# 17 of 22 gate and up pairs of each feed-forward block as 2x2 block products of seven, in a two-layer hybrid decoder

## The chip, the cores and the metric

The kernel runs on one core of one Trainium2 chip. The metric is the device time of one execution in microseconds. All data are float32; matrix products run on TensorE, elementwise work on VectorE and ScalarE, a little on GpSimd.

## The reference

512 tokens with 1024 channels go through two layers. Each layer has a feed-forward block with half weight, a mixer (state space, sliding-window attention and spatial gating side by side) and a second feed-forward block. The change is in the four feed-forward blocks alone:

```python
def rmsnorm(x, w):
    y = x * lax.rsqrt(jnp.mean(x * x, axis=-1, keepdims=True) + EPS)
    return y * w
def swiglu(x, w_gate, w_up, w_down):          # (1024, 2816), (1024, 2816), (2816, 1024)
    return (jax.nn.silu(x @ w_gate) * (x @ w_up)) @ w_down
for l in range(DEPTH):                        # DEPTH = 2
    x = x + 0.5 * swiglu(rmsnorm(x, ffn1_norm[l]), ffn1_w_gate[l], ffn1_w_up[l], ffn1_w_down[l])
    ...                                       # the mixer
    x = x + 0.5 * swiglu(rmsnorm(x, ffn2_norm[l]), ffn2_w_gate[l], ffn2_w_up[l], ffn2_w_down[l])
return rmsnorm(x, final_norm)
```

## The kernel before

The residual stays in SBUF as eight tiles xT of 128 channels by 512 tokens. A weight product takes both operands as an exact pair hi + lo of numbers of the type float32r and sums hi*hi, hi*lo and lo*hi in PSUM (`product`, lines 148, 149 and 151): three matmuls with 128 x 128 weights and 512 moving columns for each chunk of 128 input channels.

`ffn` (line 252) splits the 2816 hidden channels into 22 tiles of 128. For each one `load` brings 512 KB of gate weights and 512 KB of up weights through SyncE's queue into one of five raw buffers; `split` parts them (cast on ScalarE, line 128, subtraction on VectorE, line 129) into one of four buffers each for hi and lo. `in_products` runs one product per tile over eight chunks: gate 0, up 0, gate 1, and so on. The first three tiles go through the chunks in levels, so that the last chunks of the residual may come late. The token scale R of the norm is not in the operand: `emit` multiplies the gate's product by R (line 302), takes silu (303), multiplies by the up product (307) and at once parts the result into the pair h (312, 313). In the last block the factor 0.5 R is applied here too (309). The down product then sums the 22 chunks of h for each of eight output tiles, `scalar_tensor_tensor` applies 0.5 R (333), and the result is added to xT (334). The last block's `down_final` (702) has tokens on partitions: the residual enters by 64 matmuls with an identity (710), then groups of two hidden tiles follow (722 to 724).

What the instructions need, and which buffers they may use, is traced by a framework; a planner orders what is ready on each engine, in the order of the program, and puts in the semaphores. Each engine then works its list in order. In the first block the weights and the residual come in a pinned order, the first four weight tiles through tiles of their own (`early`). GpSimd adds the squares for the norm's statistics at the start of each block.

## Time and profile before

| | us |
|---|---|
| median of 3 runs (lowest, highest) | 1886.74 (1886.61, 1889.0) |
| profiled execution: its time, which the profile gives as the span | 1886.8 |
| TensorE busy | 1868.9 (99%) |
| weight load busy, beside it | 1527.5 (81%) |
| VectorE busy | 874.1 (46%) |
| ScalarE busy | 632.5 (34%) |
| GpSimd busy | 127.9 (7%) |

The span runs from the first instruction to the last. PE is TensorE, PEld its weight load, DVE VectorE, ACT ScalarE, POOL GpSimd, SP SyncE. Matmuls are pipelined, so their recorded durations overlap, and a busy TensorE says nothing of how fast it goes; the distance between starts does. The granted clock is a share of 2.4 GHz: 0.50 is 1.2 GHz.

### The profile page before, as it was taken

How to read it: one execution, taken by the hardware profiler on the slowest of the kernel's cores; microseconds unless marked ns; L12 is line 12 of the kernel's file. 1: busy time of each engine (PE TensorE's matmuls, PEld its weight loads, DVE VectorE, ACT ScalarE, POOL GpSimd, SP SyncE). 2: the span in 40 equal slices, each digit the busy share in tenths (PEclk: the TensorE clock that was granted, in tenths of full speed). 3: DMA queues.
4: the chain of work that ended last, by engine and by line, in shares of the span. 5: the costliest groups of instructions: out<-in, count | busy, mean ns of one | idle time of the engine just before them, and what ended most of it. 6: DMA issues, size and time to landing. Idle time of an engine off the chain costs nothing.

```text
span 1886.8 us, 21326 instructions
## 1 busy us (share of the span) xinstructions
PE 1868.9 (99%) x8608; PEld 1527.5 (81%) x8608; DVE 874.1 (46%) x1203; ACT 632.5 (34%) x854; POOL 127.9 (7%) x126
## 2 busy tenths in 40 slices
PE   8999999999999999999999999999999999999998
PEld 6888888877888888888888888887778888888886
DVE  6444433368855433433344344333787554444222
ACT  4323322247443322322223233223564432232112
POOL 2000000010221000000000000001102200000000
PEclk9999999999999999999999999999999999999999
DMA  5222333342222232233322323333422223223231
GB/s 210 100 100 90 98 92 93 97 141 70 79 87 99 91 101 99 89 92 99 102 91 99 101 91 93 92 90 110 123 89 69 90 90 101 96 94 101 79 100 45
DMA packets 54926, 182.78 MB, mean 97 GB/s; under 512 B 7211, under 2 KB 9196, under 8 KB 54828
## 3 DMA queue, kind: packets, MB, share of 16 engines
q1 hardware_dynamic: 49484, 172.37, 28.2%
q0 software_dynamic: 1920, 6.59, 1.2%
q10 hardware_dynamic: 3424, 2.46, 0.4%
q8 instruction: 68, 1.11, 0.2%
q14 instruction: 30, 0.25, 0.0%
HBM read 178.48 MB, written 2.92 MB: 96 GB/s over the span
## 4 chain that ended last, share of the span: by engine, by line
PE 94%; DVE 2%; DMA 1%; issue 1%; ACT 1%; POOL 0%; POOLq 0%; SPq 0%; ACTq 0%; DVEq 0%
PE accb L148 28%; PE accb L149 28%; PE accb L151 28%; PE mxb L723 1%; PE mxb L724 1%; PE mxb L722 1%; PE accb L723 1%; PE accb L722 1%; PE accb L724 1%; DMA acb<-arow 1%; PE mxb L179 1%; PE mxb L492 0%; PE mxb L192 0%; PE mxb L588 0%; PE mxb L641 0%
## 5 line engine op out<-in xcount | busy, mean ns | idle before, releaser
L148 PE MATMUL accb<-xhi,whi 128*128 128x512 f32 x1856 | 728.5, 393 | 5.9 <-ACT xhi L137 5.9
L149 PE MATMUL accb<-xlo,whi 128*128 128x512 f32 x1856 | 727.2, 392 | 0.5 <-DVE xlo L138 0.5
L151 PE MATMUL accb<-xhi,wlo 128*128 128x512 f32 x1856 | 726.5, 391 | 0.0
L128 ACT CAST whi<-raw 128x1024 fp32r<-128x1024 f32 (+1 forms) x322 | 333.1, 1037 | 1077.5 <-PE accb L149 619.3
L129 DVE TENSOR_TENSOR wlo<-raw,whi 128x1024 fp32r<-128x1024 f32 (+1 forms) x322 | 387.5, 1206 | 302.6 <-ACT whi L128 293.1
L148 PEld LDWEIGHTS accb<-xhi,whi 128*128 128x128 f32 x1856 | 350.0, 189 | 78.7 <-ACT xhi L137 6.1
L149 PEld LDWEIGHTS accb<-xlo,whi 128*128 128x128 f32 x1856 | 349.6, 188 | 75.1 <-DVE xlo L138 2.6
L151 PEld LDWEIGHTS accb<-xhi,wlo 128*128 128x128 f32 x1856 | 349.7, 188 | 73.1 <-issue 1.0
L148 PE MATMUL accb<-h,whi 128*128 128x512 f32 x528 | 208.0, 394 | 0.0
L151 PE MATMUL accb<-h,wlo 128*128 128x512 f32 x528 | 207.0, 392 | 0.0
L149 PE MATMUL accb<-h,whi 128*128 128x512 f32 x528 | 204.9, 388 | 0.0
L307 DVE TENSOR_TENSOR t<-accb,t 128x512 f32<-128x512 f32 x88 | 60.8, 691 | 273.3 <-PE accb L151 273.2
L302 DVE TENSOR_TENSOR t<-accb,R 128x512 f32<-128x512 f32 x88 | 60.5, 691 | 204.0 <-PE accb L151 203.9
L172 POOL TENSOR_TENSOR sqs<-sqs,sq 128x512 f32<-128x512 f32 x48 | 74.9, 1561 | 1118.9 <-ACT sq L171 1117.7
L151 PEld LDWEIGHTS accb<-h,wlo 128*128 128x128 f32 x528 | 99.1, 188 | 23.2
L149 PEld LDWEIGHTS accb<-h,whi 128*128 128x128 f32 x528 | 99.1, 188 | 22.2
L148 PEld LDWEIGHTS accb<-h,whi 128*128 128x128 f32 x528 | 99.3, 188 | 19.7
L313 DVE TENSOR_TENSOR h<-t,h 128x512 fp32r<-128x512 f32 x88 | 60.3, 685 | 3.4 <-ACT h L312 3.4
L312 ACT CAST h<-t 128x512 fp32r<-128x512 f32 x88 | 54.7, 621 | 19.1 <-DVE t L309 16.7
L303 ACT ACTIVATE t<-t 128x512 f32<-128x512 f32 x88 | 55.1, 627 | 3.8 <-DVE t L302 3.5
L333 DVE SCALAR_TENSOR_TENSOR t<-accb,R 128x512 f32<-128x512 f32 x24 | 16.6, 692 | 57.7 <-PE accb L151 57.7
L138 DVE SCALAR_TENSOR_TENSOR xlo<-xT,col,xhi 128x512 fp32r<-128x512 f32 x48 | 40.7, 866 | 2.4 <-ACT xhi L137 2.4
(203 smaller groups left out, 1088.9 us busy)
## 6 DMA issues: line engine op xcount, KB each, us to landing
raw<-in_ffn_w_gate_dram SPq DMA_DIRECT2D x86, 512.0 KB, 3.3
raw<-in_ffn_w_up_dram SPq DMA_DIRECT2D x86, 512.0 KB, 3.3
raw<-in_ffn_w_down_dram SPq DMA_DIRECT2D x48, 512.0 KB, 3.5
raw<-in_w_in_dram SPq DMA_DIRECT2D x40, 512.0 KB, 3.3
raw<-in_last_w_down_dram SPq DMA_DIRECT2D x22, 512.0 KB, 3.3
raw<-in_ffn_w_down_dram SPq DMA_DIRECT2D x24, 384.0 KB, 3.1
raw<-in_w_out_dram SPq DMA_DIRECT2D x16, 512.0 KB, 3.3
acb<-arow POOLq DMA_DIRECT2D x8, 512.0 KB, 6.1
```

Of the source, the lines that this page charges most:

```text
L128: pinned(nc.scalar.copy(out=hi[:, c], in_=raw[:, c]))
L129: pinned(nc.vector.tensor_tensor(out=lo[:, c], in0=raw[:, c], in1=hi[:, c].bitcast(F32), op=ALU.subtract))
L138: pinned(nc.vector.scalar_tensor_tensor(out=lo, in0=src, scalar=w, in1=hi.bitcast(F32), op0=ALU.mult, op1=ALU.subtract))
L148: nc.tensor.matmul(ps, whi[:, i, :], xh, start=(k == first), stop=False)
L149: mm = nc.tensor.matmul(ps, whi[:, i, :], xl, start=False, stop=(wlo is None and k == last))
L151: mm = nc.tensor.matmul(ps, wlo[:, i, :], xh, start=False, stop=(k == last))
L172: eng.tensor_tensor(out=self.s, in0=self.s, in1=q, op=ALU.add)
L302: nc.vector.tensor_tensor(out=t, in0=b, in1=R, op=ALU.mult)
L303: nc.scalar.activation(out=t, in_=t, func=AF.Silu)
L307: nc.vector.tensor_tensor(out=t, in0=b, in1=t, op=ALU.mult)
L312: nc.scalar.copy(out=hi, in_=t)
L313: nc.vector.tensor_tensor(out=lo, in0=t, in1=hi.bitcast(F32), op=ALU.subtract)
```

## The change

The normed residual and a pair of gate and up tiles form a 2 x 2 block product. The residual's blocks A have 256 tokens by 512 channels; the weights' blocks B are gate and up (128 columns each) by the two halves of the channels. Four quarter results come from seven block products of sums and differences of blocks, each of 4 chunks x 3 matmuls with 256 moving columns. The first five pairs (HEAD) stay as they were, ten plain tiles. While they run, `operands` makes the seven left factors, now with R in them, four times: for each it takes two chunks, makes sums in the scratch tile T and parts all 1792 columns. For each later pair `Seven` loads both weight tiles, makes four sums on VectorE (in T too) and parts four sources, three of 1024 columns and one of 512. The loop issues the blocks with these partings between them; the seventh block is held back until the next pair's first two blocks have gone out (`finish_last`). 0.5 R and silu go into h, which is kept as one float32 tile: eight in the block's own tiles, the rest in the 16 tiles of the residual's pairs. `split_h` parts h at the start of the down product, in the rooms that T, the operands and others leave (`room`). The down product takes its first four output tiles together, eight chunks of h at a time, and does the held-back block after the first three chunks; `down_final` does it after the first quarter of its residual. The first four weight tiles of the run use raw buffers, and the attention's bias table uses T.

```diff
-RAW, TB = 5, 3
+HEAD = 5
+KEEP = 8
...
+    def parts(src, hi, lo):
+        nc.scalar.copy(out=hi, in_=src)
+        nc.vector.tensor_tensor(out=lo, in0=src, in1=hi.bitcast(F32), op=ALU.subtract)
...
+            elif then:
+                nxt = then()
             emit(lead + n, b)
+        return nxt
...
+            def temp():
+                return ff.tile([P, 2048], F32, name="tmp", tag="T")
...
-                early = [ff.tile([P, 1024], F32, name=f"early{n}", tag=f"h{14 + n}") for n in range(4)]
+                early = [rawtile() for n in range(4)]
...
-            for f in range(KF):
+            for f in range(HEAD):
                 tiles += [maker(gv, f), maker(uv, f)]
             cur = {}
+            def htile():
+                n = len(h)
+                if n < KEEP:
+                    h.append(ff.tile([P, T], F32, name=f"h{n}", tag=f"h{n}"))
+                else:
+                    h.append(xp.tile([P, T], F32, name=f"h{n}", tag="xs", bufs=16))
+                return h[n]
...
+            lows, highs = [], []
+            def operands(c):
+                pair = ff.tile([P, 2, 7, 256], F32R, name=f"as{c}", tag=f"as{c}")
+                hi, lo = pair[:, 0], pair[:, 1]
+                v = temp()[:, 0:1792].rearrange("p (i n) -> p i n", n=256)
+                a11, a12, a22, s1, s2, s3, s4 = (v[:, i, :] for i in range(7))
+                a21 = s3
+                tt = nc.vector.tensor_tensor
+                for j, o in ((c, v[:, 0:6:5, :]), (c + 4, v[:, 1:3, :])):
+                    nc.vector.scalar_tensor_tensor(out=o, in0=xT[j].rearrange("p (s n) -> p s n", s=2),
+                                                   scalar=vcol(wrow + j), in1=R.rearrange("p (s n) -> p s n", s=2),
+                                                   op0=ALU.mult, op1=ALU.mult)
+                tt(out=s1, in0=a21, in1=a22, op=ALU.add)
+                tt(out=s3, in0=a11, in1=a21, op=ALU.subtract)
+                tt(out=s2, in0=a11, in1=s1, op=ALU.subtract)
+                tt(out=s4, in0=a12, in1=s2, op=ALU.add)
+                parts(v, hi, lo)
+                lows.append(lo)
+                highs.append(hi)
             def emit(n, b):
                 if n % 2 == 0:
-                    t = ff.tile([P, T], F32, name="t", tag="t", bufs=TB)
+                    t = ttile32()
                     nc.vector.tensor_tensor(out=t, in0=b, in1=R, op=ALU.mult)
                     nc.scalar.activation(out=t, in_=t, func=AF.Silu)
                     cur[0] = t
+                    if n >= 2 and n // 2 <= 4:
+                        operands(n // 2 - 1)
                 else:
                     t = cur[0]
                     nc.vector.tensor_tensor(out=t, in0=b, in1=t, op=ALU.mult)
-                    if fin:
-                        nc.vector.scalar_tensor_tensor(out=t, in0=t, scalar=0.5, in1=R, op0=ALU.mult, op1=ALU.mult)
-                    pair = ff.tile([P, 2, T], F32R, name=f"h{len(h)}", tag=f"h{len(h)}")
-                    hi, lo = pair[:, 0, :], pair[:, 1, :]
-                    nc.scalar.copy(out=hi, in_=t)
-                    nc.vector.tensor_tensor(out=lo, in0=t, in1=hi.bitcast(F32), op=ALU.subtract)
-                    h.append((hi, lo))
+                    nc.vector.scalar_tensor_tensor(out=htile(), in0=t, scalar=0.5, in1=R, op0=ALU.mult, op1=ALU.mult)
                     if first and len(h) == 2:
-                        attention_bias(ff, ("h13", "h12", "h11"))
+                        bias = temp()
+                        attention_bias(lambda i: bias[:, i * 512:(i + 1) * 512])
...
-            in_products(tiles, xs, emit, {(3, 1) if first else (1, 0): st.start, (3 if first else 1, "R"): make},
-                        [[0, 1], [2, 3], [4, 5], [6, 7]] if first else None, feed, 3 if first else 2)
+            class Seven:
+                def __init__(self, f):
+                    self.g, self.u = load(gv[f]), load(uv[f])
+                def sums(self):
+                    self.t = temp()
+                    b11, b21, b12, b22 = (t[:, i:i + 512] for t in (self.g, self.u) for i in (0, 512))
+                    t1, t2, t3, t4 = (self.t[:, i * 512:(i + 1) * 512] for i in range(4))
+                    tt = nc.vector.tensor_tensor
+                    tt(out=t1, in0=b12, in1=b11, op=ALU.subtract)
+                    tt(out=t2, in0=t1, in1=b22, op=ALU.subtract)
+                    tt(out=t3, in0=b22, in1=b12, op=ALU.subtract)
+                    tt(out=t4, in0=b21, in1=t2, op=ALU.add)
+                    self.srcs = [self.g, self.t[:, 0:1024], self.t[:, 1024:2048], self.u[:, 512:1024]]
+                    self.his, self.los = [], []
+                def hi(self):
+                    i = len(self.his)
+                    hi = wtile("whi") if i < 3 else ff.tile([P, 512], F32R, name="uhi", tag="uhi")
+                    nc.scalar.copy(out=hi, in_=self.srcs[i])
+                    self.his.append(hi)
+                def lo(self):
+                    i = len(self.los)
+                    lo = wtile("wlo") if i < 3 else ff.tile([P, 512], F32R, name="ulo", tag="ulo")
+                    nc.vector.tensor_tensor(out=lo, in0=self.srcs[i], in1=self.his[i].bitcast(F32), op=ALU.subtract)
+                    self.los.append(lo)
...
+            def seven(f):
+                w = Seven(f)
+                w.sums()
+                for i in range(4):
+                    w.hi()
+                    w.lo()
+                return w
+            def block(ps, wt, s, start, stop):
+                whi, wlo = wt
+                for c in range(4):
+                    xh, xl = highs[c][:, s, :], lows[c][:, s, :]
+                    nc.tensor.matmul(ps, whi[:, c, :], xh, start=(start and c == 0), stop=False, skip_group_check=True)
+                    nc.tensor.matmul(ps, whi[:, c, :], xl, start=False, stop=False, skip_group_check=True)
+                    mm = nc.tensor.matmul(ps, wlo[:, c, :], xh, start=False, stop=(c == 3), skip_group_check=True)
+                latest[0] = mm.ins
+            A11, A12, A22, S1, S2, S3, S4 = range(7)
+            Q0, Q1 = slice(0, 256), slice(256, 512)
+            last = []
+            def finish_last(between=lambda: None):
+                while last:
+                    x, wt4, t, hv = last.pop()
+                    block(x, wt4, A22, False, True)
+                    nc.scalar.activation(out=t[:, Q1], in_=x, func=AF.Silu)
+                    between()
+                    nc.vector.scalar_tensor_tensor(out=hv, in0=t, scalar=0.5, in1=hv, op0=ALU.mult, op1=ALU.mult)
+            nxt = in_products(tiles, xs, emit, {(3, 1) if first else (1, 0): st.start, (3 if first else 1, "R"): make},
+                              [[0, 1], [2, 3], [4, 5], [6, 7]] if first else None, feed, 3 if first else 2,
+                              then=lambda: seven(HEAD))
+            add = nc.vector.tensor_tensor
+            for f in range(HEAD, KF):
+                w, nxt = nxt, Seven(f + 1) if f + 1 < KF else None
+                do = lambda what: getattr(nxt, what)() if nxt else None
+                x, z, y = accbank()[:, Q0], bank()[:, Q0], bank()[:, Q0]
+                p1, p5, u2 = (ff.tile([P, 256], F32, name=n, tag=n) for n in ("p1", "p5", "u2"))
+                t, hv = ttile32(), htile()
+                do("sums")
+                block(x, w.part(0), A11, True, True)
+                nc.scalar.copy(out=p1, in_=x)
+                block(z, w.part(1), S1, True, True)
+                nc.scalar.copy(out=p5, in_=z)
+                if last:
+                    finish_last(lambda: (do("hi"), do("lo")))
+                else:
+                    do("hi"), do("lo")
+                block(x, w.part(1, 1), S2, False, True)
+                nc.scalar.copy(out=u2, in_=x)
+                do("hi"), do("lo")
+                block(y, w.part(0, 1), A12, True, True)
+                do("hi")
+                add(out=t[:, Q0], in0=y, in1=p1, op=ALU.add)
+                do("lo")
+                nc.scalar.activation(out=t[:, Q0], in_=t[:, Q0], func=AF.Silu)
+                block(z, w.part(3), S4, False, True)
+                do("hi")
+                add(out=hv[:, Q0], in0=z, in1=u2, op=ALU.add)
+                do("lo")
+                block(x, w.part(2), S3, False, True)
+                add(out=hv[:, Q1], in0=x, in1=p5, op=ALU.add)
+                last.append((x, w.part(2, 1), t, hv))
+            def room():
+                t = ff.tile([P, 2048], F32R, name="hp", tag="T")
+                for i in range(4):
+                    yield t[:, i * 512:(i + 1) * 512]
...
+            free = room()
+            hs = []
+            def split_h(upto):
+                while len(hs) < min(upto, KF):
+                    hs.append((next(free), next(free)))
+                    parts(h[len(hs) - 1], *hs[-1])
+            split_h(3)
             if fin:
-                down_final(dv, h)
+                down_final(dv, hs, split_h, finish_last)
                 return
-            for j in range(KD):
-                b = accbank()
-                for k in range(0, KF, 8):
-                    kc = min(8, KF - k)
-                    wt = split(load(dv[l, j, :, k * P:(k + kc) * P]))
-                    product(b, wt, h, [(i, k + i) for i in range(kc)], 0, KF - 1)
-                t = ff.tile([P, T], F32, name="t", tag="t", bufs=TB)
-                nc.vector.scalar_tensor_tensor(out=t, in0=b, scalar=0.5, in1=R, op0=ALU.mult, op1=ALU.mult)
-                nc.vector.tensor_tensor(out=xT[j], in0=xT[j], in1=t, op=ALU.add)
+            steps = [(j, k) for k in range(0, KF, 8) for j in range(LEAD)]
+            steps += [(j, k) for j in range(LEAD, KD) for k in range(0, KF, 8)]
...
+            for n, (j, k) in enumerate(steps):
...
+                if n == 0:
+                    product(bs[j], wt, hs, ks[:3], 0, KF - 1)
+                    finish_last()
+                    split_h(8)
+                    ks = ks[3:]
+                product(bs[j], wt, hs, ks, 0, KF - 1)
+                if n + 1 < len(steps):
+                    nxt = dw(*steps[n + 1])
+                if n < 8:
+                    split_h(8 + 2 * (n + 1))
+                if k + kc == KF:
+                    add_x(j, bs[j])
...
-        bs = [[bank(), bank()], [bank(), bank()], [accbank(), accbank()], [accbank(), accbank()]]
+        bs = []
         for c in range(NB):
+            new = bank if c < 2 else accbank
+            bs.append([new(), new()])
             for j in range(KD):
                 nc.tensor.matmul(bs[c][j // 4][:, (j % 4) * P:(j % 4 + 1) * P], xT[j][:, c * P:(c + 1) * P], ident,
                                  start=(j % 4 == 0), stop=False)
+            if c == 0:
+                finish_last()
         groups = [(f, f + 1) for f in range(0, KF, 2)]
         for fs in groups:
             ws = [split(load(dv[f]), D) for f in fs]
+            split_h(fs[0] + 4)
```

## Rows read from the trace of the kernel before

**Rows 1.** The page's shares and granted clock (slices; 9 is 90% or more).

```profile
PE 1868.9 (99%) x8608; PEld 1527.5 (81%) x8608; DVE 874.1 (46%) x1203; ACT 632.5 (34%) x854; POOL 127.9 (7%) x126
...
PEclk9999999999999999999999999999999999999999
```

**Rows 2.** The page's chain of waits that ended last, by engine.

```profile
PE 94%; DVE 2%; DMA 1%; issue 1%; ACT 1%; POOL 0%; POOLq 0%; SPq 0%; ACTq 0%; DVEq 0%
```

**Rows 3.** The page's costliest group: count, busy us, mean ns, idle before, releaser.

```profile
L148 PE MATMUL accb<-xhi,whi 128*128 128x512 f32 x1856 | 728.5, 393 | 5.9 <-ACT xhi L137 5.9
```

**Rows 4.** Timeline of TensorE, gate and up: start us, duration us, what.

```profile
100.09 0.39 PE L148 MATMUL accb<-xhi,whi 128*128 128x512 f32 x1
100.32 0.39 PE L149 MATMUL accb<-xlo,whi 128*128 128x512 f32 x1
100.54 0.39 PE L151 MATMUL accb<-xhi,wlo 128*128 128x512 f32 x1
```

**Rows 5.** Stretches: length; PE, PEld, DVE, ACT, POOL busy; clock; DMA share, GB/s.

```profile
60.00:235.00 175.00, 175.00 (x774) 144.91 (x773) 71.67 (x81) 51.85 (x65) 0.00 (x0) 1.00 0.29 96
...
1347.00:1350.30 3.30, 3.30 (x10) 2.63 (x9) 3.30 (x6) 2.78 (x4) 1.05 (x2) 0.50 0.00 0
```

**Rows 6.** Timeline of VectorE, gate and up; idle before and releaser in brackets.

```profile
228.81 0.69 DVE L302 TENSOR_TENSOR t<-accb,R 128x512 f32<-128x512 f32 x1 [2.71 <-PE accb L151]
...
234.32 0.69 DVE L307 TENSOR_TENSOR t<-accb,t 128x512 f32<-128x512 f32 x1 [3.38 <-PE accb L151]
235.16 1.23 DVE L129 TENSOR_TENSOR wlo<-raw,whi 128x1024 fp32r<-128x1024 f32 x1
236.30 0.68 DVE L313 TENSOR_TENSOR h<-t,h 128x512 fp32r<-128x512 f32 x1
239.69 0.69 DVE L302 TENSOR_TENSOR t<-accb,R 128x512 f32<-128x512 f32 x1 [2.71 <-PE accb L151]
```

**Rows 7.** Timeline of weight loads, the same stretch as rows 4.

```profile
100.09 0.19 PEld L149 LDWEIGHTS accb<-xlo,whi 128*128 128x128 f32 x1
```

**Rows 8.** Timeline of weight loads behind four transposes in the mixer.

```profile
465.11 0.59 PEld L450 LDWEIGHTS mxb<-ident,xs 128*128 128x128 f32 x4
465.67 0.19 PEld L148 LDWEIGHTS accb<-xhi,whi 128*128 128x128 f32 x1
465.78 0.19 PEld L149 LDWEIGHTS accb<-xlo,whi 128*128 128x128 f32 x1
```

**Rows 9.** Timeline of TensorE, float32 products by the identity.

```profile
1749.82 3.73 PE L710 MATMUL mxb<-ident,xT 128*128 128x128 f32 x32
```

**Rows 10.** VectorE's groups by line and shape: columns as in rows 3.

```profile
L129 DVE TENSOR_TENSOR wlo<-raw,whi 128x1024 fp32r<-128x1024 f32 x298 | 364.5, 1226 | 217.3 <-ACT whi L128 207.8 <-PE mxb L192 0.5
...
L313 DVE TENSOR_TENSOR h<-t,h 128x512 fp32r<-128x512 f32 x88 | 60.3, 685 | 3.4 <-ACT h L312 3.4
L138 DVE SCALAR_TENSOR_TENSOR xlo<-xT,col,xhi 128x512 fp32r<-128x512 f32 x48 | 40.7, 866 | 2.4 <-ACT xhi L137 2.4
...
L129 DVE TENSOR_TENSOR wlo<-early,whi 128x1024 fp32r<-128x1024 f32 x3 | 4.7, 1579 | 0.0
...
L563 DVE SCALAR_TENSOR_TENSOR s<-mxb,bm 128x256 f32<-128x256 f32 x4 | 1.5, 415 | 0.0
```

**Rows 11.** ScalarE's groups by line and shape: columns as in rows 3.

```profile
L128 ACT CAST whi<-raw 128x1024 fp32r<-128x1024 f32 x298 | 312.9, 1053 | 972.5 <-PE accb L149 519.0 <-issue 371.5 <-PE accb L723 64.4
...
L312 ACT CAST h<-t 128x512 fp32r<-128x512 f32 x88 | 54.7, 621 | 19.1 <-DVE t L309 16.7 <-DVE t L307 2.4
...
L584 ACT COPY pT<-mxb 128x256 f32<-128x256 f32 x4 | 1.4, 360 | 0.0
```

**Rows 12.** Timeline of TensorE, the longest idle stretch of the mixers.

```profile
1345.53 0.44 PE L588 MATMUL mxb<-pT,vt 128*64 128x128 f32 x4 [2.06 <-ACT pT L584]
```

**Rows 13.** The page's DMA issues: count, KB each, us to landing.

```profile
raw<-in_ffn_w_gate_dram SPq DMA_DIRECT2D x86, 512.0 KB, 3.3
```

More of the change, by code (lines that the diff above doesn't have):

```diff
@@ L121, in split @@
         m = raw.shape[1]
-        hi = wp.tile([P, 1024], F32R, name="whi", tag="whi", bufs=4)[:, :m]
-        lo = wp.tile([P, 1024], F32R, name="wlo", tag="wlo", bufs=4)[:, :m]
+        hi, lo = wtile("whi")[:, :m], wtile("wlo")[:, :m]
         for i in range(2 if mid else 1):
@@ new lines, in add_x @@
+            def add_x(j, b):
+                nc.vector.tensor_tensor(out=xT[j], in0=b, in1=xT[j], op=ALU.add)
+            LEAD = 4
+            steps = [(j, k) for k in range(0, KF, 8) for j in range(LEAD)]
+            steps += [(j, k) for j in range(LEAD, KD) for k in range(0, KF, 8)]
+            bs = {}
+            nxt = dw(*steps[0])
+            for n, (j, k) in enumerate(steps):
+                wt = nxt
+                kc = min(8, KF - k)
+                if j not in bs:
+                    bs[j] = accbank()
+                ks = [(i, k + i) for i in range(kc)]
+                if n == 0:
[10 more added lines that the diff above has]
+                    add_x(j, bs[j])
```

46 lines of the change are left out of this document (35 added, 11 removed).

## The prediction

> **What bounds the kernel now.** I read the page's shares first. TensorE is busy for 99% of 1886.8 us at the full clock, VectorE for 46%, ScalarE for 34% [rows 1]. The chain of waits is 94% TensorE [rows 2], so what TensorE no longer does shortens the run, unless another wait ends last in its place. The costliest group is the products with the normed residual, three lines of 1856 matmuls each [rows 3]. Their mean of 393 ns is not their price, because matmuls are pipelined. The price is the distance from one start to the next: in the timeline starts lie 0.22 to 0.23 us apart [rows 4], and in a stretch of gate and up alone 774 matmuls, two of them cut by the stretch's edge, fill 175 us, 0.2267 us each [rows 5]. A pair is 2 x 8 x 3 = 48 of them, 10.88 us, and VectorE's rows say the same: the multiplication of a gate tile by R comes at 228.81 and again at 239.69 [rows 6]. There VectorE waits 2.7 to 3.4 us for each tile's last matmul, so TensorE ends last. The profiled execution has a span of 1886.8 us and no other time of its own; the median of the runs is 1886.74, so the sum needs no offset.
>
> **The change, part by part.**
>
> *Fewer columns on TensorE.* 17 pairs in each of four FFNs, 68 in all, cost 68 x 10.88 = 740 us. A pair becomes 7 blocks x 4 chunks x 3 = 84 matmuls of 256 columns: 84 x 256 columns for 48 x 512, an eighth less, but 1.75 times the instructions, each with a weight load of its own. No row shows a matmul of this type with 256 columns, so I bound it.
> - From below: while a matmul streams, the next weights load; the load starts with the matmul [rows 4, 7]. Where nothing streams for long, loads of this type follow each other by 0.11 us (465.67, 465.78), and four transposes' loads fit in 0.59 [rows 8]. The nearest row in balance is the float32 product by the identity: 128 x 128, a load for each record, 32 records in 3.73 us, (3.73 - 0.27)/31 = 0.112 us [rows 9]. The stream alone gives 0.2267/2 = 0.113. So 0.112.
> - From above: 512 columns at 2.4 GHz are 0.2133 us, so 0.0134 of 0.2267 is extra. If that is paid once for each matmul, 256 columns cost 0.1067 + 0.0134 = 0.120. If it also stands behind a full load, 0.112 + 0.0134 = 0.126.
>
> I take 0.116, between 0.112 and 0.120, the two readings of the plain stream. A pair then takes 84 x 0.116 = 9.74 us, 1.14 less, and 68 pairs give 77 us. The ends: 100 us at 0.112, 55 at 0.120, 20 at 0.126. The gain is gone at 10.88/84 = 0.1295.
>
> *What must be ready beside it.* VectorE does for each pair four sums of 512 columns, three subtractions of 1024 and one of 512, three additions of 256 out of PSUM and one closing product of 512: 4 x 0.685 + 3 x 1.226 + 0.685 + 3 x 0.415 + 0.685 = 9.03 us [rows 10], where the old pair took about 4.5. ScalarE casts 3 x 1024 and 512 columns and moves five pieces of 256: 3 x 1.053 + 0.621 + 5 x 0.360 = 5.6 us [rows 11]. Both fit under 9.74, VectorE barely; durations of neighbours overlap by some 0.09 us (one of 1.23 begins at 235.16, the next operation at 236.30 [rows 6]), so its own pace is nearer 8. The buffers set the order. Three of four whi tiles are live and the fourth holds the former pair's third, which is free only when the held-back block ends as third of the seven (3 x 1.39 us). The next pair's casts can start at 4.2, 5.6, 7.0 and 8.4 us and their subtractions end near 6.6, 8.0, 9.4 and 10, while the first two are wanted at 9.7 and 11.1: some 3 us of cover. Each accumulator that is copied out (p1, p5, u2) is written again only two blocks later, 2.8 us against a copy of 0.36. I charge nothing here; without the cover a late chain would cost up to 1 us a pair.
>
> *The step from plain tiles to sevens.* Called 0 is the end of the ninth plain tile. Behind it VectorE runs the emission (0.7), then the last chunk's operands: two scaled copies (2 x 0.866), four sums (4 x 0.415), a cast of 1792 columns on ScalarE (1.7, by the slope of its 1024 and 512 rows) and its subtraction (2.0, by the same slope) [rows 10, 11], ending at about 7.5. TensorE finishes the tenth tile at 5.4, begins the first block and needs that chunk at its end. The sums of the first seven share the operands' scratch tile, so they begin at 7.5 and end at 9.9; the second block's low part is ready at about 11, where TensorE could have used it at 7 to 8. So it stands some 3 us. In the trace, where TensorE had stood for 2.06 us at 1343.5 [rows 12], the granted clock read 0.50 soon after, for 1347.0 to 1350.3 [rows 5], 1.2 instead of 2.4 GHz; half of 3.3 us is 1.7 more. 4 x 4.7 = 19 us, between 4 (other casts fill the wait, the clock holds) and 40.
>
> *h is parted later.* The cast (0.62) and subtraction (0.685) of h leave the pairs and go into the down product. Tiles 0 to 2 can be parted while the last seven runs. Tile 3 goes into the room of the operands, which the held-back block still reads: it runs after 9 matmuls of the down product, so tile 3 comes 0.62 + 0.685 after it and TensorE waits about 1.3, taken as 1.5, and then each further h costs VectorE 0.685 against 3 x 0.2267 = 0.68. 3 x 1.5 = 4.5 us; the last FFN covers it with 64 products by the identity. Between 0 and 4 us each.
>
> *Edits at nothing.* Half and R now enter in one operation before the down product instead of after it: off the chain before and after. The first four weight tiles stand in four of the five raw buffers, so the next loads start later; a load lands in 3.3 us [rows 13] and each plain tile lasts 24 x 0.2267 = 5.4 us, which covers it; if not, it costs at most the 3.3 us. The bias table shares the operands' scratch tile in the first FFN: VectorE alone waits, 0 to 2 us.
>
> Sum: 1886.8 - 77.4 + 19 + 4.5 = 1833.
>
> **The rivals.**
>
> *VectorE or its chain ends last.* For it: 9.03 of 9.74 us, in-order queues, one scratch tile. Against: 3 us of cover and gaps of 2.7 to 3.4 us in the rows of now. If each pair loses 0.7 us to such waits, the pair takes 10.44 and the run 1886.8 - 30 + 23 = 1880. At the loaded rate at the start (1024 columns in 1.579, 512 in 0.866) [rows 10] it is 3 x 1.579 + 6 x 0.866 + 3 x 0.415 = 11.2 us, 20 us slower, with the steps 1930; but those are the three first weight tiles of the run, and of 298 later ones the mean is 1.226. It turns slower from a pair of 10.5 us on.
>
> *The extra stands behind the load.* At 0.126 the gain is 20 us and the steps take it: 1890, no change. For it: the 0.0134 has no explanation in the trace. Against: a float32 record with equal stream and load shows 0.112, so no such sum.
>
> *The load is not hidden: slower.* If a 256-column matmul's successor loads only when it has left the array, the price is 0.113 + 0.110 = 0.223 us, the pair 18.73 us, the run 1886.8 + 68 x 7.85 + 23 = 2444; it decides from 0.1295 on, a sixth of a load uncovered. Against it: in the rows of now a load starts with the matmul before it [rows 4, 7], and at 0.112 [rows 9] stream and load cannot lie one after the other. The Trainium skill (TensorE: Matmul & The Clock Gate, Part 3, The mechanism) says that weight loads overlap matmuls in flight only where they use different row groups; that would give this rival. By that rule pairs would not be overlapped now either, and this trace's start times disagree.
>
> **How the numbers follow.** The forecast has 0.68: 1795 (0.112, small steps) to 1867 (0.120, steps of 35). VectorE's chain has 0.14, in half of it faster; the extra behind the load 0.12, a third of it faster; the uncovered load 0.06. The predicted time is the forecast's 1833. The range 1794 to 1884 leaves out the uncovered load, the bad half of VectorE's case and most of the 0.126 case, near 0.2 in all. A difference under 0.2%, 3.8 us, is about what a measurement of this kernel can tell from none. Faster: 0.67 + 0.07 + 0.04 = 0.78; within 0.2%: 0.05; slower: 0.17.
>
> **What would show it.** In a stretch of sevens alone, starts 0.112 to 0.120 us apart at clock 1.00 and a pair period of 9.4 to 10.1 us; VectorE's busy share there near 0.9 and TensorE without gaps inside a pair; one gap of 2 to 4 us at each step to the sevens and one of 1 to 2 us at three steps to the down product; plain tiles still at 0.2267. It is wrong if starts lie 0.1295 or more apart, if TensorE waits for wlo or the sums inside every pair, or if the gaps at the steps add up to over 40 us.

## The result, and the profile after

The changed kernel takes 1844.16 us (median of four runs, 1842.94 to 1845.56), the one before 1886.67 beside it (1886.05 to 1889.0): a ratio of 0.9773 [0.976, 0.9786], 2.3% faster. The forecast was 1833, with a range of 1794 to 1884. The traced execution took 1842.94 with a span of 1841.2, against a span of 1886.8 before, so the two traces have 45.6 us between them to explain. The medians lie only 42.5 apart: the traced execution of the changed kernel was the fastest of its four, and that of the kernel before a longer one than usual, since in the runs beside e1 executions of 1886.8 to 1887.1 us have spans of 1885.1 to 1885.4. Three executions far off all others are left out of every median here (4844 us of the kernel before, 2328 of e2, 2781 of e4), and of e2 only that one was traced, at a granted clock of 0.75.

The page of the changed kernel: shares and clock (columns as in [rows 1]), the chain by engine [rows 2], and two of the costliest groups [rows 3].

```profile
PE 1810.8 (98%) x11056; PEld 1600.8 (87%) x11056; DVE 1225.7 (67%) x1833; ACT 840.4 (46%) x1278; POOL 130.5 (7%) x126
...
PEclk9899999999999999999999999999999999999999
...
PE 88%; DVE 7%; ACT 2%; DMA 2%; issue 1%; POOL 0%; POOLq 0%; SPq 0%; ACTq 0%; DVEq 0%
...
L163 PE MATMUL accb<-xhi,whi 128*128 128x512 f32 x784 | 310.6, 397 | 6.2 <-ACT xhi L152 6.2
L419 PE MATMUL accb<-as,whi 128*128 128x256 f32 x1088 | 308.8, 284 | 4.2 <-ACT as L126 4.2
```

TensorE is still the bound: 2448 more matmuls in less time, VectorE up from 46% to 67%. Of the 1856 plain matmuls of line L148, 784 remain (now L163). One slice of the clock, near the start, reads 8 instead of 9: there the granted clock was lower for a while.

The price of a matmul of the sevens is again read from starts, not from the mean of 284 ns. TensorE's timeline of the changed kernel, gate and up (start us, duration us, what):

```profile
100.05 0.28 PE L421 MATMUL accb<-as,wlo 128*128 128x256 f32 x1
100.17 0.28 PE L419 MATMUL accb<-as,whi 128*128 128x256 f32 x1
100.29 0.28 PE L420 MATMUL accb<-as,whi 128*128 128x256 f32 x1
```

Every distance is 0.12 us; of 5704 between neighbouring matmuls of the sevens, 5610 are 120 ns. The Trainium skill (TensorE: Matmul & The Clock Gate, Part 2, Back-to-back issue gap) gives 262 cycles for 256 columns, 109 ns at 2.4 GHz, and names no type for it; for float32r the rows say 120, and the measurement decides.

A pair is therefore 84 x 0.120 = 10.08 us. VectorE's timeline of the changed kernel, the subtraction of the first whi in two neighbouring pairs, and the windows of 100 us of sevens (columns as in [rows 5]):

```profile
1088.50 1.23 DVE L399 TENSOR_TENSOR wlo<-raw,whi 128x1024 fp32r<-128x1024 f32 x1 [1.85 <-ACT whi L393]
...
1098.58 1.23 DVE L399 TENSOR_TENSOR wlo<-raw,whi 128x1024 fp32r<-128x1024 f32 x1 [1.85 <-ACT whi L393]
...
1000.00:1100.00 100.00, 100.00 (x836) 100.00 (x835) 81.69 (x121) 53.48 (x90) 0.00 (x0) 1.00 0.33 106
```

The period is 10.08 us (before: 10.88 [rows 6]), TensorE has no gap, and VectorE is busy for 82 of 100 us (the prediction expected near 90), 8.2 us of a pair, with one idle stretch of 1.85. The prediction's pace of nearly 8 us, read from overlapping durations, was the right one, not its sum of 9.03.

The steps from plain tiles to sevens: TensorE's timeline in the first FFN, then at another one (idle and releaser in brackets).

```profile
71.33 0.28 PE L421 MATMUL accb<-as,wlo 128*128 128x256 f32 x1
75.81 0.58 PE L419 MATMUL accb<-as,whi 128*128 128x256 f32 x1 [4.20 <-ACT as L126]
...
77.87 0.58 PE L420 MATMUL accb<-as,whi 128*128 128x256 f32 x1 [1.48 <-DVE as L127]
...
982.88 0.28 PE L421 MATMUL accb<-as,wlo 128*128 128x256 f32 x1
984.78 0.39 PE L419 MATMUL mxb<-as,whi 128*128 128x256 f32 x1 [1.62 <-ACT whi L393]
```

Three FFNs (feed-forward blocks) have one idle stretch of 1.62 us. The first has 4.20 us, and right behind it a slow stretch, inside which 1.48 and, near 81 us, 2.26 more are idle. The window of it:

```profile
75.80:86.00 10.20, 6.45 (x26) 5.87 (x27) 9.69 (x11) 3.50 (x5) 0.00 (x0) 0.50 0.32 104
```

The granted clock there is 0.50, the lower level of 1.2 GHz, from the end of the 4.20 idle us up to 86.0 us; behind the single gaps of 1.62 us the matmuls keep their 0.12. VectorE's timeline in the first FFN says why TensorE stands so long, and next to it the same step in another FFN:

```profile
53.62 1.42 DVE L343 SCALAR_TENSOR_TENSOR tmp<-xT,col,R 128x512 f32<-128x512 f32 x2 [1.67 <-DMA skew<-tmp]
...
75.78 2.03 DVE L127 TENSOR_TENSOR as<-tmp,as 128x1792 fp32r<-128x1792 f32 x1 [1.75 <-ACT as L126]
...
979.64 2.02 DVE L127 TENSOR_TENSOR as<-tmp,as 128x1792 fp32r<-128x1792 f32 x1 [1.95 <-ACT as L126]
```

The second of the four `operands` waits for the transfer that reads the bias table out of the shared scratch tile. The 1.67 us are only the last part: the table has the tile from 41.4 us, when the first operands are done with it, to 53.6, and where the table lies elsewhere the second operands begin at 43.09 (e3). All that VectorE does behind them is late: the last subtraction starts 4.45 us after TensorE's last matmul (71.33 to 75.78), in the other FFN 3.24 us before it (979.64 to 982.88).

The step to the down product, TensorE's timeline, and ScalarE's first cast of h there:

```profile
1155.42 0.39 PE L166 MATMUL accb<-hp,wlo 128*128 128x512 f32 x1
1155.65 0.28 PE L419 MATMUL accb<-as,whi 128*128 128x256 f32 x1
...
1156.96 0.28 PE L421 MATMUL accb<-as,wlo 128*128 128x256 f32 x1
1157.08 0.63 PE L163 MATMUL accb<-hp,whi 128*128 128x512 f32 x2
...
1156.20 1.66 ACT L126 CAST hp<-h 128x512 fp32r<-128x512 f32 x3 [1.20 <-PE accb L421]
```

No idle. The cast begins at 1156.20, while the held-back block still runs (1155.65 to 1157.08): a quarter of the room is free as soon as its own three matmuls are done. And at 1157.08 two matmuls of line L163 follow each other, where elsewhere L164 comes next: the planner has put one of other work in between (which, the trace does not say). The four starts from 1157.08 on take 1.10 us instead of 0.91, so some 0.2 us are lost.

Last, a gain that nobody asked for: the products with h. Windows of 100 us (columns as in [rows 5]) with such products alone, of the first down product (upper line) and of the last product (lower line), first before the change and then after it:

```profile
260.00:360.00 100.00, 100.00 (x439) 82.04 (x438) 34.38 (x38) 27.06 (x32) 7.70 (x5) 1.00 0.30 91
1770.00:1870.00 100.00, 100.00 (x430) 80.58 (x429) 20.09 (x18) 16.00 (x16) 0.00 (x0) 1.00 0.22 69
```
```profile
260.00:360.00 100.00, 100.00 (x443) 82.81 (x442) 39.01 (x47) 31.84 (x44) 8.52 (x5) 1.00 0.32 95
1730.00:1830.00 100.00, 100.00 (x443) 82.84 (x442) 21.58 (x21) 18.80 (x24) 0.55 (x1) 1.00 0.19 64
```

439 and 430 matmuls became 443 and 443. From the first start to the last, the 528 matmuls with h of the last product take 123.05 us before and 119.59 after, and those of each other down product 120.64 and 119.68 (without the held-back block between them).

By stages the 45.6 us are: 68 pairs, 54.4 less; steps to the sevens, 17.7 more; steps to the down product, 0.2 each, counted with the down products; down and last products, 6.3 less. What remains, 2.6 less, is no stage's gain that the traces show: the two traced executions lie 3.1 us further apart than the medians.

### The profile page after: what moved, and what is told of

The parts are those of the page before. It is cut to its first block, busy times and chain, and to the rows that moved or that the text cites. A ratio compares the mean times of both kernels' runs of the same rounds, so it can differ in the third digit from the quotient of the medians.

```text
span 1841.2 us, 27456 instructions
## 1 busy us (share of the span) xinstructions
PE 1810.8 (98%) x11056; PEld 1600.8 (87%) x11056; DVE 1225.7 (67%) x1833; ACT 840.4 (46%) x1278; POOL 130.5 (7%) x126
## 4 chain that ended last, share of the span: by engine, by line
PE 88%; DVE 7%; ACT 2%; DMA 2%; issue 1%; POOL 0%; POOLq 0%; SPq 0%; ACTq 0%; DVEq 0%
PE accb L163 13%; PE accb L164 13%; PE accb L166 13%; PE accb L419 7%; PE accb L420 7%; PE accb L421 7%; PE mxb L419 5%; PE mxb L421 5%; PE mxb L420 5%; DVE as L127 1%; PE mxb L925 1%; PE mxb L924 1%; PE mxb L923 1%; PE accb L925 1%; PE accb L924 1%
## 5 line engine op out<-in xcount | busy, mean ns | idle before, releaser
L144 DVE TENSOR_TENSOR wlo<-raw,whi 128x1024 fp32r<-128x1024 f32 (+2 forms) x191 | 226.7, 1192 | 264.0 <-ACT whi L143 262.9
L163 PE MATMUL accb<-xhi,whi 128*128 128x512 f32 x784 | 310.6, 397 | 6.2 <-ACT xhi L152 6.2
L419 PE MATMUL accb<-as,whi 128*128 128x256 f32 x1088 | 308.8, 284 | 4.2 <-ACT as L126 4.2
L164 PE MATMUL accb<-xlo,whi 128*128 128x512 f32 x784 | 309.4, 395 | 0.5 <-DVE xlo L153 0.5
L420 PE MATMUL accb<-as,whi 128*128 128x256 f32 x1088 | 308.3, 283 | 1.5 <-DVE as L127 1.5
L421 PE MATMUL accb<-as,wlo 128*128 128x256 f32 x1088 | 308.1, 283 | 0.0
L166 PE MATMUL accb<-xhi,wlo 128*128 128x512 f32 x768 | 302.3, 394 | 0.0
L419 PEld LDWEIGHTS accb<-as,whi 128*128 128x128 f32 x1088 | 209.2, 192 | 5.2 <-ACT as L126 4.4
L420 PEld LDWEIGHTS accb<-as,whi 128*128 128x128 f32 x1088 | 209.2, 192 | 2.0 <-DVE as L127 1.8
L421 PEld LDWEIGHTS accb<-as,wlo 128*128 128x128 f32 x1088 | 209.1, 192 | 0.0
L164 PE MATMUL accb<-hp,whi 128*128 128x512 f32 x528 | 205.8, 390 | 0.0
L163 PE MATMUL accb<-hp,whi 128*128 128x512 f32 x528 | 205.0, 389 | 0.0
L163 PEld LDWEIGHTS accb<-xhi,whi 128*128 128x128 f32 x784 | 146.6, 187 | 37.6 <-ACT xhi L152 6.4
L164 PEld LDWEIGHTS accb<-xlo,whi 128*128 128x128 f32 x784 | 146.4, 187 | 34.4 <-DVE xlo L153 2.6
L419 PE MATMUL mxb<-as,whi 128*128 128x256 f32 x544 | 155.2, 286 | 7.1 <-ACT whi L393 7.1
L420 PE MATMUL mxb<-as,whi 128*128 128x256 f32 x544 | 154.6, 284 | 0.0
```

Of the source, the lines that this page charges most:

```text
L144: pinned(nc.vector.tensor_tensor(out=lo[:, c], in0=raw[:, c], in1=hi[:, c].bitcast(F32), op=ALU.subtract))
L163: nc.tensor.matmul(ps, whi[:, i, :], xh, start=(k == first), stop=False)
L164: mm = nc.tensor.matmul(ps, whi[:, i, :], xl, start=False, stop=(wlo is None and k == last))
L166: mm = nc.tensor.matmul(ps, wlo[:, i, :], xh, start=False, stop=(k == last))
L419: nc.tensor.matmul(ps, whi[:, c, :], xh, start=(start and c == 0), stop=False, skip_group_check=True)
L420: nc.tensor.matmul(ps, whi[:, c, :], xl, start=False, stop=False, skip_group_check=True)
```

## Experiments

Four questions: what sets the 120 ns (a fixed extra for each matmul, or something about the addresses); whether the products with h gained by an address; whether the scratch tile and the order of work make the steps; and how far VectorE is from its limit. Ratios are to the kernel before, run on the same chip.

**e1, the matmul alone.** It computes nothing of the reference: stretches of 72 float32r matmuls out of one large tile, 8 chunks of three products, three times.

```
for r in range(3):
    for k in range(8):
        matmul(ps, whi_k, xhi_k); matmul(ps, whi_k, xlo_k); matmul(ps, wlo_k, xhi_k)   # n columns
```

> Stretches of 72 float32r matmuls alone, both operands 320 bytes past a multiple of 512 as in the kernels; nothing of the reference is computed. Theory A, a fixed price for each matmul: start distances are columns / 2.4 + 13.4 ns, so 227 ns at 512 columns, 200 at 448, 173 at 384, 147 at 320, 120 at 256, and at 192 and 128 the weight load's 108 to 112 ns; 64 or 32 weight columns at 256 moving columns leave 120. Theory B, the stream slows in proportion and at 256 columns the load ends last: 198 at 448, 170 at 384, 142 at 320, 120 at 256 with 128 weight columns but 113 with 64 or 32. Theory C, the extra comes from the operands' addresses: where both lie on a multiple of 512 bytes it is 216 at 512 columns and 109 at 256; A and B expect 227 and 120 there. Shifting one operand alone by 64 bytes: 229 to 233 at 512 columns if the relative address matters, 227 if not.

The stretches' groups (shortest, median and longest duration in ns; first and last start in us, for one of the three lines), with 128 weight columns where the form does not say 128*64; "whalf" has 64, "wshift" and "halfwshift" have their weights 64 bytes further:

```profile
L84 PE MATMUL nfull<-big x24: 388/389/390, 34.2 to 49.9; 128*128 128x512 f32 x24
L84 PE MATMUL nthreequarter<-big x24: 333/334/343, 65.1 to 77.1; 128*128 128x384 f32 x24
L84 PE MATMUL nhalf<-big x24: 281/284/284, 88.2 to 96.5; 128*128 128x256 f32 x24
L84 PE MATMUL whalf<-big x24: 275/276/280, 112.9 to 120.7; 128*64 128x256 f32 x24
L84 PE MATMUL wshift<-big x24: 391/394/395, 170.7 to 186.8; 128*128 128x512 f32 x24
L84 PE MATMUL halfwshift<-big x24: 276/276/286, 294.4 to 302.2; 128*128 128x256 f32 x24
```

Last start less first, over 69 distances, is about the price; from the single records, once a stretch has settled, it is 226.7 ns at 512 columns, 202.6 at 448, 173.3 at 384, 146.7 at 320, 120.0 at 256, then 111.7 at 192 and 128. From 512 to 256 that is n/2.4 plus 13.3, as theory A has it (but for 448, where 15.9 are left over); below, something else of 111.7 ends last. So B's slower stream is out, and C too: with both operands on a multiple of 512 bytes 512 columns took 226.7 and 256 took 120.0. Thus a fixed extra gives the kernel's 120, though what it is, no run shows. It isn't always paid, either: 256 columns with 64 weight columns took 113.3 (where A had 120 and B 113), and with weights displaced also 113.3. Repeating the weights left 120. At 512 columns a moving operand 64 bytes further costs 228.9, weights so displaced 233.3, both displaced alike 226.7, the moving operand or both by 256 bytes 226.7: what counts is how the two stand to each other, not where either stands.

**e2, the address alone.** One small tile of the kernel before, named in three places, gets the size that it has in the changed one, which moves all that lies behind it, h included. Nothing else differs.

```
...
-            r = rp.tile([P, NB], F32, name="rcol", tag="rcol", bufs=2)
+            r = rp.tile([P, P // 2], F32, name="rcol", tag="rcol", bufs=2)[:, 0:NB]
...
```

> The kernel before, with one edit of the change alone: the small tile of the norm's column takes 256 bytes instead of 16, which moves every tile allocated after it, so that h lies 320 bytes past a multiple of 512 as the weights do. Theory: the 1 us that each down product and the 3.3 us that the last one lost in the change come from this, 3 x 1.0 + 3.3 = 6.3 us, so 1880.4 us. Rival: they come from parting h later; then 1886.7.

1880.96 us, ratio 0.9964 [0.995, 0.9978], 6.1 less than the 1887.04 beside it. The stretches of the first down product and of the last product in its trace, whose clock is 0.75 throughout:

```profile
1480.00:1580.00 100.00, 100.00 (x354) 70.10 (x354) 30.01 (x34) 23.16 (x28) 6.79 (x5) 0.75 0.25 73
2190.00:2290.00 100.00, 100.00 (x354) 70.24 (x353) 16.53 (x14) 13.98 (x14) 0.00 (x0) 0.75 0.18 58
```

354 and 354 matmuls, where the kernel before has 439 and 430: the two products now have one pace. So the 6.3 us of the down and last products are an address, not the algorithm. Their size fits e1: for 528 matmuls they are 1.8 and 6.6 ns each, where displaced operands cost 2.2 or 6.6.

**e3, the bias table out of the scratch tile.**

```
-                        bias = temp()
-                        attention_bias(lambda i: bias[:, i * 512:(i + 1) * 512])
+                        attention_bias(lambda i: ff.tile([P, T], F32, name="bias", tag=f"h{7 - i}"))
```

> The changed kernel with the attention's bias table in the rooms of h5, h6 and h7 instead of the operands' scratch tile. Theory: in the first block the operands waited for the table's transfers, which made the step to the sevens 9.3 us longer than in the other three (11.4 against 2.1); without it 1844.2 - 9.3 = 1834.9 us, and no stretch at half clock after the start. Rival: the first block's vector work is late for other reasons (its own start); then the step stays at 9 to 11 us and the time at 1842 to 1844.

1836.05 us, 0.9728 [0.9714, 0.9742], 8.1 under the change. The second operands begin 10.5 us earlier (43.09 against 53.62; VectorE's timeline, upper line), and the first step is now like the others, by its only longer idle stretch (TensorE's, lower line):

```profile
43.09 0.74 DVE L343 SCALAR_TENSOR_TENSOR tmp<-xT,col,R 128x512 f32<-128x512 f32 x1
...
74.86 0.39 PE L418 MATMUL mxb<-as,whi 128*128 128x256 f32 x1 [1.65 <-ACT whi L392]
```

Of the 9.3 us expected 1.2 are missing. Not as expected, the clock still reads 0.5 once, from 38.0 to 41.5 us, ahead of the step; why, no run shows.

**e4, one plain tile pair more ahead of the sevens.** `HEAD = 5` becomes `HEAD = 6`, so 16 pairs are sevens.

> The changed kernel with six plain pairs instead of five, and 16 sevens, in each block; the operands are still made behind the second to fifth gate tiles, so one plain pair more stands between the last operands and the first seven. Theory, the step's wait is the chain of operands and sums: it goes in three blocks (3 x 2.1) and nearly all of it in the first (some 10), while four sevens fewer give back 4 x 0.80 = 3.2: 1844.2 - 16.3 + 3.2 = 1831 us. Rival, the wait belongs to the first seven itself (its own casts and sums): it stays, and the time is 1844.2 + 3.2 = 1847.

1830.65 us, 0.9704 [0.9685, 0.9722]. Four pairs fewer cost 4 x 0.80 = 3.2 us, yet it is 13.5 faster: the steps are worth about 16.7, as the theory had it (16.3). The two longest waits left on TensorE (engine, tile and line, releaser: us in total, times, longest) are those of the first plain tile and of a mixer, none of a seven:

```profile
PE accb L163 <- ACT xhi L152: 5.9, 1, 5.9
PE mxb L778 <- DVE s L775: 2.8, 2, 1.4
```

**e5, more stretches.** As e1, with other shapes and displacements (x: the moving operand, w: the weights).

```
("halfsixtyfour", 256 columns, w + 64 bytes), ("fivesmall", 320, 64 weight columns), ("threesmall", 384, 64 weight columns), ...
```

> Stretches of matmuls alone again, nothing of the reference is computed. In the first such run 256 columns took 120.0 ns with weights and moving operand at the same remainder of 256 bytes, 113.3 with the weights 64 bytes on or with 64 weight columns. Theory D: a stream of n float32r columns takes n x 17/16 cycles of 2.4 GHz (113.3 ns at 256, 141.7 at 320, 170 at 384, 226.7 at 512), and what lies above it is a load and a stream at the same remainder meeting each other; only the difference of the two addresses counts. Then the moving operand 64 bytes back gives 113.3 as well, 64 weight columns give 141.7 at 320, 170 at 384 and 226.7 at 512, and with the weights 64 bytes on 320 and 384 columns come near 142 and 170. Theory A, a fixed price for each matmul of 13.3 ns that only 256 columns escape: 146.7 and 173.3 with either, and 220 or less at 512 with 64 weight columns. Shifts by 16 and 32 bytes are open: between 113 and 120 at 256 columns, 227 to 233 at 512.

```profile
L82 PE MATMUL halfsixtyfour<-big x24: 281/281/282, 67.9 to 76.0; 128*128 128x256 f32 x24
...
L82 PE MATMUL fivesmall<-big x24: 304/309/310, 101.6 to 111.7; 128*64 128x320 f32 x24
L82 PE MATMUL threesmall<-big x24: 333/333/339, 122.7 to 134.6; 128*64 128x384 f32 x24
```

At 320 and 384 columns fewer weight columns change nothing (146.7, 173.3), against theory D, and at 512 they take 230.0, against both. At 256 columns displaced operands give 113.3 (x 64 bytes back) or 117.8, and w + 64 gave 117.8 here where e1, at the same addresses, gave 113.3; by 16, 32 and 128 bytes it is 118.3 to 118.6. Neither law holds at 256 columns. At 512, x 64 back and w 64 on both give 233.3, x 64 on and w 192 on both 228.9, which bears out a period of 256 bytes.

**e6, the operands of the sevens displaced by 64 bytes in the changed kernel.**

```
-                pair = ff.tile([P, 2, 7, 256], F32R, name=f"as{c}", tag=f"as{c}")
+                room = ff.tile([P, 64 + 3584], F32R, name=f"as{c}", tag=f"as{c}")
+                pair = room[:, 48:3632].rearrange("p (e i n) -> p e i n", e=2, n=256)
```

> The changed kernel with the parted operands of the sevens 64 bytes further back against the weights (their tiles get 256 bytes more and are entered 192 bytes in); nothing else moves. Theory D: 5712 matmuls at 113.3 instead of 120.0 ns, 38.1 us less, so 1844.2 - 38.1 = 1806 us and start distances of 113 to 114 ns in the sevens. Theory A, a fixed price for each matmul: 1844 us. Rival: VectorE's 8.2 us busy in a pair of 10.08 leave too little in one of 9.52, and part of the gain turns into waits inside the pairs: 1815 to 1830.

1818.14 us, 0.964 [0.9595, 0.9685], with runs from 1809.06 to 1831.33: more scatter than any other kernel here. The traced execution is the one of 1831.33. Two windows of it, 90 us each:

```profile
700.00:790.00 90.00, 90.00 (x766) 90.00 (x765) 74.67 (x110) 49.06 (x82) 0.00 (x0) 1.00 0.35 108
...
1600.00:1690.00 90.00, 90.00 (x796) 90.00 (x796) 76.42 (x113) 51.77 (x87) 0.00 (x0) 1.00 0.37 112
```

766 matmuls in the second FFN and 796 in the fourth; from the single records 117.8 and 113.3 ns from start to start. At one set of addresses the matmul has two prices. The time lies in the range of the rival, but the rival's waits are not there: TensorE is busy for 90.00 of 90 us in both windows, VectorE for 75 and 76. In this execution only the fourth FFN has the lower price throughout; that the shorter executions had it in more FFNs is likely, but they were not traced.

**e11, what decides between the two.** As e1: the same displaced stretch of 256 columns (x 64 bytes back) behind stretches of different kinds.

```
("full", 512, aligned), ("xminusfulla", 256, x - 64), ("half", 256, aligned), ("xminushalfa", 256, x - 64), ...
```

> Stretches of matmuls alone, nothing of the reference is computed: the same displaced pair of addresses again and again (moving operand 64 bytes back, and weights 64 bytes on) behind 512 columns, behind 256 at one remainder and behind 64 weight columns. Open since the last runs: the same addresses gave 113.3 ns in one run and 117.8 in another. Theory E, what ran before sets it: every repeat behind the same kind of stretch gives the same of the two. Theory F, it is drawn anew at each start or for a whole execution: both appear behind one kind, or one value throughout, whatever stood before.

```profile
L105 PE MATMUL xminusfulla<-big x24: 281/281/281, 50.3 to 58.4; 128*128 128x256 f32 x24
...
L105 PE MATMUL xminushalfa<-big x24: 276/276/286, 141.8 to 149.6; 128*128 128x256 f32 x24
```

Behind 512 aligned columns it is 117.8, four times of four; behind 256 aligned ones (120) 113.3, four of four; behind 256 with 64 weight columns (113.3) 117.8, three of three. With the weights displaced instead, behind 512 columns, it was 117.8 four times of four. So for these stretches theory E holds, in one execution: what ran before sets the pace, and the stretch of 72 keeps it.

**e9, own scratch for the operands.** With e3's idea (rooms h5, h4, h3), without e6's shift.

```
-KEEP = 8
+KEEP = 6
-                v = temp()[:, 0:1792]...
+                v = ff.tile([P, 1792], F32, name="own", tag="own")...
+                t = ff.tile([P, 1792], F32R, name="hp", tag="own")   # three rooms for h
```

> The changed kernel with the bias table in rooms of h and a scratch tile of their own for the operands (two h tiles fewer in the block's own room); operands of the sevens at their old addresses, so 120 ns each. Theory, the first seven's sums wait for the scratch tile that the last operands hold: the 2.1 us that each of four steps loses go, most of 8, against the kernel with the bias table moved alone (1836.1), so 1828 to 1830 us and no wait of 1.6 us at the steps. Rival, VectorE is late there with the operands themselves: 1836.

1827.95 us, 0.9682 [0.9667, 0.9696], as the theory had it. The sums of the first seven no longer wait for the last operands, and no step is idle: the two longest waits left on TensorE are again those of the first plain tile and of a mixer.

```profile
PE accb L163 <- ACT xhi L152: 6.0, 1, 6.0
PE mxb L780 <- DVE s L777: 1.9, 2, 1.0
```

**e7, e9 with e6's shift**, and **e8, e3 and e4 with e6's shift.**

> The shift, the bias table in rooms of h, and a scratch tile of their own for the operands (two h tiles fewer in the block's own room), five plain pairs. Theory: 1836.1 - 38.1 for the shift, and the 1.6 us of waiting for the first seven's sums go at four steps, 6.5 us: 1791 to 1792 us. Rival, the sums stand behind the operands on VectorE anyway: the steps stay and it is 1798.

> The shift, the bias table in rooms of h and six plain pairs with 16 sevens, the operands' scratch tile shared as in the change. Theory: 1831.6 - 5376 x 6.67 ns = 1795.7 us; the bias table's own room adds nothing, since a plain pair more already covered it. With the pair of a seven at 9.52 us, four sevens fewer cost 4 x 1.36 us against the kernel with own scratch, whose steps are then the question.

e7: 1794.03 us, 0.9521 [0.9487, 0.9556], the fastest of all, with runs from 1789.74 to 1804.28; the time can't tell its theory from its rival, but no step in its trace is idle. e8: 1820.03, 0.9647 [0.9632, 0.9661], 24 us over its expectation. The windows of sevens, e7 first:

```profile
1000.00:1100.00 100.00, 100.00 (x885) 100.00 (x884) 85.39 (x126) 56.80 (x96) 0.00 (x0) 1.00 0.38 112
```
```profile
1000.00:1100.00 100.00, 100.00 (x851) 100.00 (x850) 82.97 (x122) 54.97 (x92) 0.00 (x0) 1.00 0.34 106
```

885 matmuls against 851: e7's sevens run at 113.3 ns, e8's at 117.8, and 5376 times the 4.5 ns between them are the 24 us. Where they part, the single records show. In all FFNs of the traces of e6, e7 and e8 the sevens begin at 117.8, behind tiles of 512 columns, as in e11. In e8 no distance above 0.12 us follows until the last pair, and the 117.8 stay. In each FFN of e7 TensorE breaks its step by 0.04 to 0.13 us a few times in the first 40 matmuls, and a few matmuls behind the last of these breaks it is 113.3, and stays so up to the last pair; such a break in the first FFN, TensorE's timeline:

```profile
74.37 0.28 PE L420 MATMUL mxb<-as,whi 128*128 128x256 f32 x1
74.53 0.38 PE L419 MATMUL accb<-as,whi 128*128 128x256 f32 x1
74.75 0.28 PE L420 MATMUL accb<-as,whi 128*128 128x256 f32 x1
```

In e6 the step's wait of 1.64 us is followed by 113.3 in three FFNs, but some ten matmuls behind a break in the next pair two of them go back to 117.8 and one does not. So what ran before covers small breaks too, and their outcome is not the same each time.

**e10, VectorE doubled where it is densest.** The four sums of each seven are made twice in the changed kernel.

```
+                    tt(out=t1, in0=b12, in1=b11, op=ALU.subtract)   # and t2, t3, t4 again
```

> The changed kernel with the four sums of each seven made twice, 4 x 0.61 = 2.4 us more on VectorE for each pair, nothing else. In the trace of the change VectorE is busy for 8.2 of 10.08 us of a pair and waits 1.85 us once, for a cast. Theory, VectorE is the second limit and nothing but its sum counts: 8.2 + 2.4 = 10.65 us a pair, 68 x 0.57 = 39 us more, 1883 us. Rival, the order of the buffers has the cover of 3 us that the prediction gave, and some of the casts and sums can still slide under the neighbouring pairs: under 1860. Rival, a chain already sits at its edge: over 1900.

1877.91 us, 0.9945 [0.9928, 0.9961], 33.8 more than the change. A window, VectorE's timeline of neighbouring pairs, and the wait of TensorE at the step of the second FFN with the window behind it:

```profile
1050.00:1100.00 50.00, 49.74 (x410) 49.13 (x409) 50.00 (x78) 26.24 (x45) 0.00 (x0) 1.00 0.34 103
...
1080.07 0.68 DVE L383 TENSOR_TENSOR tmp<-raw 128x512 f32<-128x512 f32 x1
...
1090.50 0.68 DVE L383 TENSOR_TENSOR tmp<-raw 128x512 f32<-128x512 f32 x1
...
644.95 0.58 PE L423 MATMUL mxb<-as,whi 128*128 128x256 f32 x1 [4.63 <-ACT whi L397]
...
645.00:651.20 6.20, 6.20 (x28) 6.08 (x29) 6.20 (x8) 2.68 (x4) 0.00 (x0) 0.50 0.44 164
```

Late in an FFN VectorE is busy for 50.00 of 50 us and the pair takes 10.43: there VectorE has become the bound. But the first pairs behind the step still take 10.08; only from the eighth on it is 10.43, which makes some 14 us in four FFNs. The larger part, 18.6 us, stands at the steps: the gaps in front of the second block grow from 7.1 to 18.7 us in all, and in three FFNs one of 4.63 us comes with a clock of 0.50 for 6.8 us. So the theory is right for the late pairs, where the 1.85 us of slack were the whole reserve (four more sums at their pace of 0.60 ask for 2.4), and the first rival for the early ones, where the cover holds. The prediction's rival of VectorE's chain is real, one such amount of work away.

## Why the prediction was right, and where not

*Right in its mechanism.* TensorE stayed the bound, no gap within a pair, all loads hidden, plain tiles still at 0.2267. The uncovered load is refuted: at 113 to 120 ns, with loads of some 110 each [rows 8], they cannot lie one after another, and the rule that the prediction quoted from the Trainium skill (TensorE: Matmul & The Clock Gate, Part 3, The mechanism) does not describe these rows.

*The mis-sized term is the price of a matmul of 256 columns.* I took 0.116, the middle of two readings of the plain stream; it was 0.120, the upper one: the extra of 512 columns is paid once for each matmul of 256, too (e1). The term became 54.4 us instead of 77.4. That is 23 us more; the steps (1.3), h (4.5) and the addresses (6.3) took 12 of it back, so the median came 11 us above 1833. That it came so near is in part luck: no term had the addresses, and the step's 19 us came out right from parts that were wrong (below). The rival "extra behind the load" (0.126) was not seen: no settled stretch of 256 columns took more than 120.

*VectorE's chain.* Costed at nothing, and within the pairs so it was; e10 shows how near its end is.

*The step to the sevens.* 19 us predicted, 17.7 measured, but put together otherwise. I had four equal steps of 3 us idle and 1.7 for the clock. Three had 1.62 of idle and no drop, 2.1 us each by stages; the first cost 11.4, of which 9.3 is the bias table on the scratch tile, which I had put among the edits at nothing ("VectorE alone waits, 0 to 2 us"). That is the step of the working that failed: the table kept the tile, the second operands began 10.5 us later than without it, and TensorE was idle for 7.9 us and had the lower clock from 75.8 to 86.0 (e3: 8.1 us back). The row of 2.06 us idle followed by a half clock [rows 12, 5] doesn't carry over to a lone gap of 1.62.

*h parted later.* 4.5 us predicted, some 0.2 at each of three steps measured. I let tile 3 wait for the whole held-back block and a chain behind it. The room comes free chunk by chunk, and the planner puts a matmul of other work in between.

*Not foreseen: 6.3 us from addresses.* The small tile's new size is in the diff; that it moves h against the weights I did not weigh (e2).

*Open.* Why displaced 256-column matmuls run at 113.3 or 117.8 is not settled, nor what the 13.3 ns are. What ran before decides in e11, and in e6 and e7 the pace changes behind breaks of a small part of a microsecond, but no run varies such a break alone. e7's gain over e9 (34 us) rests on it: the kernel may fall to e8's pace with another neighbouring edit.

## What to carry to other kernels

An eighth fewer columns is not an eighth less time: price the matmul by start distances at the new width, with the fixed part charged to every instruction, before trading long for short ones. Where a scratch tile gets a second user, count how long that user keeps it, transfers included, and follow the delay through the in-order queue to the engine that needs the last product: the wait that shows (1.7 us) was the end of a stay of 12, and it cost 9. Give critical tiles their own room, and look where matmul operands lie to each other when a tile's size changes.

## What the runs showed of the hardware that was not expected

- A float32r matmul costs n/2.4 ns and 13.3 more at 512, 384, 320 and 256 columns (226.7 to 120.0; at 448 15.9 more), and not less than 111.7 at 192 and 128 columns (e1).
- The places of weights and moving operand relative to each other, with a period of 256 bytes, change that: at 512 columns 226.7 when equal, up to 233.3 when not; at 256 columns 120.0 when equal, 113.3 or 117.8 when 64 bytes apart (e1, e5).
- Of the last two, the one that holds depends on what TensorE ran before (e11); it can last for a whole FFN (e7, e8), and it can change behind a break of about 0.1 us (e6, e7).
- An idle stretch of 4.20 us was followed by a clock of 0.50 from 75.8 to 86.0 us, and ones of 4.63 us came with 0.50 for 6.8 us (e10); single ones of 1.62 us in the same place did not.
